# A hybrid decoder layer on one core: the chunked recurrence run as two chains without fill matmuls between its products

## The chip, the cores and the metric

The kernel runs on one core of a Trainium2 chip. The metric is the device time of one execution in microseconds (us), less is better. TensorE is shown as PE (matmuls) and PEld (weight loads), VectorE as DVE, ScalarE as ACT, GpSimd as POOL, SyncE as SP.

## What is computed

One layer of a decoder trunk for 512 prompt tokens and 32 sample tokens (8 requests of 4 tokens), model width 1024, all in fp32. Cut to what matters:

```python
x = layer_norm(ALPHA * x + 0.5 * swiglu(x, ffn1...), ln1)
proj = x @ w_in                      # r, k, v, gates for 8 heads of 64; b, c, h of the convolution
# RWKV-7, per head, token by token:
sa = einsum("bhij,bhj->bhi", s, -kk_t)
s  = s * w_t[:, :, None, :] + sa[..., None] * (kk_t * a_t)[:, :, None, :] + v_t[..., None] * k_t[:, :, None, :]
o_t = einsum("bhij,bhj->bhi", s, r_t)
# group norm of o per head, plus a bonus term, times a gate; next to it a gated convolution of width 3
mix = concat([y_rwkv, y_conv]) @ w_out
x = layer_norm(ALPHA * x + mix, ln2)
x = layer_norm(ALPHA * x + 0.5 * swiglu(x, ffn2...), ln3)
```

The sample tokens start from a given state `s` per request; the prompt starts from zero. The final states of both are outputs, next to y.

## The kernel before

**Fill work.** The large products (`mm3`, L145 to L153) split both operands into a high and a low fp32r part and issue three matmuls for each 128x128 block of weights, L149 to L151, over 256 or 288 token columns (the halves of the 544 tokens). A 128x1024 weight tile is split by ACT (L133) and DVE (L134). These products are written as generators that yield after every two blocks. A deque `bg` holds the generators that are waiting, and `take(need)` (L157) draws from its front until the yielded costs add up to `need`. `weave(key, crit)` runs a critical generator and, each time that it yields a cost, takes `FILL[key]` times that cost from `bg`. So the fill's products stand on TensorE's queue between those of the critical generator; `until`, `need` and `drain` take fill until a condition is met or the deque is empty. The engines run their instructions in the order in which a scheduler has put them from this program order.

**The recurrence.** It is written in chunks of 64 tokens. Eight heads form four pairs, and two pairs a group `g`; in a pair, the heads `par` = 0 and 1 lie on partitions 0 to 63 and 64 to 127 (`R(par)`), and `pl` is the pair's place in the group. For each group:

- `Pair.scores` (L888) forms the products of each chunk's keys with themselves and with the queries (into `SC`), transposes keys and values (into `BK` and `UV`), and writes the 64x64 blocks to memory (`Ad`).
- `elim(g)` (L933) inverts the triangular 64x64 blocks. The 16x16 diagonal blocks of all chunks are inverted by 15 short steps on DVE (L951, L953), after a round trip through memory that regroups them, and sent back through memory (L956 to L960). Then four rounds of small products (L987) build the whole inverse `XT`; each round has three pieces (chunks 0 to 3, 4 to 7, and the sample), and after each piece the generator yields 300, so that fill is woven in. After round 0, POOL copies `AR` into `SC` (L1013).
- `chain(g)` (L1018) goes through the eight chunks in order. Both pairs share a PSUM tile at each step: products of `SC` with the state S (L1033, L1035), a copy W by ACT (L1037), products with `XT` (L1048), copies into `UV` by DVE (L1049) and ACT (L1050), products with `BK` (L1055). Then DVE adds the old state (L1064) and multiplies by the chunk's decay `Pe` (L1066), for each of the two partition halves. The outputs come from L1043 and L1071 and are copied to `O` by ACT (L1073). Three times a chunk the generator yields 1000.
- `sample(g)` (L1077) does the same for the 32 sample tokens: 32 products of eight columns for S0 times `AR` (L1089), three small groups (L1103, L1110, L1117), and the update of the eight states by four products of 128x512 (L1127), each behind a masked copy `ux` by DVE (L1124), followed by two DVE operations of 128x512 per pair (L1129, L1130).
- `gnorm(g, h)` (L1134) normalizes half h of the output, with fp32 products at L1143, L1148 and L1160.

**The order of the stages** (L1254 to L1396). With fill woven in throughout: the scores of pairs 0 and 1, `elim(0)` (key e0; pair 3's projections are put into the deque behind the DVE steps), chain 0 (c0) with `sample(0)` alternating with the fill, the two halves of `gnorm(0)`, the scores of pairs 2 and 3, `elim(1)` (e1), chain 1 in parts (c1, c2, c3) with `sample(1)`, with the output projection's products (`wout(0)`, `last(0)`), with the second half of the convolution (`conv_last`) as fill, and with the first half of the second layer norm beside its last steps. The second feed-forward part follows.

Of the kernel before, what the change touches and what calls it, by code (L numbers as in the profile page):

```python
# [19 lines left out]
P = 128  # L20
# [26 lines left out]
FILL = dict(l1a=1.754, l1b=0.752, p0=9022, s0=0.93, p1=5506, s1=1.832, e0=0.658, c0=0.233, g0=0.399, s2=0.531, p3=425, s3=0.85, e1=0.392, c1=0.963, c2=0.734, c3=0.8, l2a=1.0, l2b=1.4, l3a=1.35)  # L47
# [14 lines left out]
def body(ctx: ExitStack, tc: tile.TileContext, xT, gu1, wd1, win, wo_c, wo_0, wo_1, gu2, wd2, lora, w0, vec, cst,  # L62
# [92 lines left out]
    bg = deque()  # L155

    def take(need):  # L157
        while need > 0 and bg:
            g = bg[0]
            try:  # L160
                need -= next(g)
            except StopIteration:
                bg.popleft()
# [630 lines left out]
    BK = tl([P, 2, 2, NC_, 64], F32, name="BK")  # L794
# [10 lines left out]
    POOL.memset(XT, 0.0)  # L805
    Ad = dr.tile([2, 16, 65, 64], F32, name="Ad")
# [6 lines left out]
    class Pair:  # L813
# [74 lines left out]
        def scores(self):  # L888
            p, pl, bkb, nk, vf = self.p, self.pl, self.bkb, self.nk, self.v
            AR, bv = ARs[p // 2], bvs[p // 2]  # L890
# [13 lines left out]
            for a0c, n in ((0, 5), (5, 4)):  # L904
                qs = (sm(), sm())
                for c in range(n):
                    for par, q in enumerate(qs):
                        PE.transpose(q[:, c * 64:(c + 1) * 64],
                                     bkb[R(par), a0c + c, par:par + 2, :].rearrange("p s t -> p (s t)"), ident[R(par), :])
                for par, q in enumerate(qs):  # L910
                    ACT.activation(BK[:, pl, par, a0c:a0c + n, :], s64(q[:, :64 * n]), AF.Copy)
                qs = (sm(), sm())
                for c in range(n):
# [6 lines left out]
                    PE.transpose(qs[1][R(0), d], vf[R(1), t:t + 64], ident[R(1), :])  # L920
                for par, q in enumerate(qs):
                    o = R(1 - par)
                    ACT.activation(UV[o, pl, par, a0c:a0c + n, :], s64(q[o, :64 * n]), AF.Copy)
                yield 500
# [8 lines left out]
    def elim(g, mid=None):  # L933
# [6 lines left out]
        dma(AT, diag(Ad))  # L940
        POOL.memset(De, 0.0)
# [22 lines left out]
        yield 15000 if g else 6000  # L964
        pieces = (range(0, 4), range(4, 8), range(8, 9))
        for rnd in range(4):
            for x in pieces:
# [22 lines left out]
                if rnd == 0:  # L990
                    for pr in (slice(0, 32), slice(64, 96)) if sam else (slice(0, P),):
                        ACT.activation(DM[pr, cc, :, 0:nn], qv[pr], AF.Copy)
                    yield 300
                    continue
                if rnd == 1 and not sam:
                    DVE.tensor_copy(XT[:, cc, :, 0:16], DT[:, cc, :, 0:16])
                    DVE.tensor_tensor(XT[:, cc, :, 16:64], qv, DT[:, cc, :, 16:64], op=OP.add)
                    yield 300
# [10 lines left out]
                yield 300  # L1009
# [8 lines left out]
    def chain(g, cp):  # L1018
        S = Sn = None
        tl = cp.tile  # L1020
        AR = ARs[g]
        for c in range(8):
            if c < 7:
                Sn = tl([P, 2, 2, 64], F32, name="S", bufs=2)
                for par in range(2):
                    POOL.tensor_copy(Sn[R(1 - par), :, par, :], UV[R(1 - par), :, par, c + 1, :])
            q = sm()
            for pl in range(2):
                for par in range(2):
                    dst = q[R(par), pl * 64:pl * 64 + 64]  # L1030
                    if c == 0:
                        o = R(1 - par)
                        PE.matmul(dst, SC[o, pl, par, c, 0:64], UV[o, pl, par, c, :], start=True, stop=True)  # L1033
                    else:
                        PE.matmul(dst, SC[:, pl, par, c, 0:64], S[:, pl, par, :], start=True, stop=True)  # L1035
            W = tl([P, 2, 64], F32, name="W", bufs=2)
            ACT.activation(W, v2(q), AF.Copy)  # L1037
            yield 1000
            q2 = sm()
            if c:  # L1040
                for pl in range(2):
                    for par in range(2):
                        PE.matmul(q2[R(par), pl * 64:pl * 64 + 64], S[R(par), pl, par, :], AR[R(par), pl, c, 1, :],  # L1043
                                  start=(pl == 0), stop=False, skip_group_check=True)
            q = sm()
            for pl in range(2):
                for par in range(2):
                    PE.matmul(q[R(par), pl * 64:pl * 64 + 64], XT[R(par), c, pl, :], W[R(par), pl, :], start=True, stop=True)  # L1048
            DVE.tensor_copy(UV[R(0), :, 0, c, :], v2(q, R(0)))  # L1049
# [430 lines left out]
```

## Time and profile before

| | us |
|---|---|
| median of 3 runs | 1111.46 (1110.05 to 1112.29) |
| profiled execution, whole | 1113.33 |
| its span, first to last instruction | 1111.6 |
| TensorE (PE) occupied | 1096.3 |
| DVE / ACT / POOL busy | 835.6 / 590.4 / 172.9 |
| mean granted TensorE clock | 0.994 of full |
| inverse of group 0 (L987) | 489.4 to 511.4 |
| chain 0 with its sample part | 511.4 to 556.9 |
| inverse of group 1 | 614.9 to 635.0 |
| chain 1 with its sample part | 635.0 to 692.0 |

The page gives the busy time of each engine, the slices of the span, and the chain of work that ended last. A window of the trace lists busy time and number of instructions of each engine in a stretch, the clock that TensorE was granted (1.00 is full speed) and what the DMA engines did. A row of the timeline is start, length, engine, line, operation, output and inputs, shapes and count; in brackets the idle time of the engine before it and what ended it. The records of TensorE overlap: a matmul's record begins before its predecessor's has ended, so the distance of two starts is what one costs when they are dense.

### The profile page before, as it was taken

Reading aid. Unit: us, or ns where it says so; the run is one execution under the profiler, and the core shown is the slowest. Engines: PE = TensorE matmul, PEld = TensorE weight load, DVE = VectorE, ACT = ScalarE, POOL = GpSimd, SP = SyncE. Lnnn points to the kernel's source line nnn. Section 1 sums busy time; section 2 is a strip of 40 time slices with the busy share of each in tenths; the row PEclk is TensorE's granted clock in tenths of the full one; section 3 lists DMA queues with packets and bytes.
Section 4 is the critical chain, followed back from the end, with each engine's and each line's share of the span. In section 5 each row is a group of like instructions: output and inputs, shape, how many; then the busy total and the mean of one; then the engine's idle time right before and its main releaser. Section 6 shows DMA issues by size and latency. Waiting matters only on the chain.

```text
span 1111.6 us, 22987 instructions
## 1 busy us (share of the span) xinstructions
PE 1096.3 (99%) x9330; PEld 1044.8 (94%) x9330; DVE 835.6 (75%) x1555; ACT 590.4 (53%) x1084; POOL 172.9 (16%) x283
## 2 busy tenths in 40 slices
PE   8999999999999999999999999999999999999997
PEld 8999999999999999898789878999999999999996
DVE  7797888889766757754578467887988888897665
ACT  6646555564543585652345334767555555645524
POOL 0131221312100022230000200001212213121000
PEclk9999999999999999998999999999999999999999
DMA  8567594967752342251137522553675949677402
GB/s 284 127 137 188 121 222 100 212 148 162 179 136 88 95 135 68 53 124 58 42 97 199 151 75 82 171 171 77 131 191 125 223 98 211 152 155 183 119 1 81
DMA packets 99370, 149.32 MB, mean 134 GB/s; under 512 B 35264, under 2 KB 60736, under 8 KB 99264
## 3 DMA queue, kind: packets, MB, share of 16 engines
q1 hardware_dynamic: 72064, 111.67, 32.5%
q0 software_dynamic: 27200, 36.18, 21.1%
q8 instruction: 73, 1.20, 0.4%
q14 instruction: 33, 0.27, 0.1%
HBM read 129.17 MB, written 9.75 MB: 125 GB/s over the span
## 4 chain that ended last, share of the span: by engine, by line
PE 83%; issue 6%; DVE 3%; DMA 3%; ACT 3%; POOL 1%; SPq 0%; POOLq 0%; DVEq 0%; ACTq 0%
PE mm L149 10%; PE mm L151 9%; PE mm L150 9%; PE mm L508 8%; PE mm L509 8%; PE mm L510 7%; PE sm L510 6%; PE sm L509 5%; PE sm L508 5%; PE sm L987 1%; DMA z<-sv 1%; PE sm L149 1%; PE sm L150 1%; PE sm L151 1%; DMA z<-cpb 1%
## 5 line engine op out<-in xcount | busy, mean ns | idle before, releaser
L134 DVE TENSOR_TENSOR hl<-raw,hl 128x1024 fp32r<-128x1024 f32 (+3 forms) x232 | 270.6, 1172 | 72.6 <-ACT hl L133 71.8
L133 ACT ACTIVATE hl<-raw 128x1024 fp32r<-128x1024 f32 (+3 forms) x232 | 232.0, 1013 | 78.6 <-DVE raw L475 38.0
L149 PE MATMUL mm<-xhl,hl 128*128 128x288 f32 (+1 forms) x736 | 225.2, 306 | 0.3 <-DVE z L1354 0.3
L150 PE MATMUL mm<-xhl,hl 128*128 128x288 f32 (+1 forms) x736 | 214.8, 292 | 0.0
L151 PE MATMUL mm<-xhl,hl 128*128 128x288 f32 (+1 forms) x736 | 214.6, 292 | 0.2 <-DVE hl L134 0.2
L149 PEld LDWEIGHTS mm<-xhl,hl 128*128 128x128 f32 x736 | 138.8, 189 | 8.5 <-issue 2.6
L151 PEld LDWEIGHTS mm<-xhl,hl 128*128 128x128 f32 x736 | 138.6, 189 | 4.0 <-issue 1.6
L150 PEld LDWEIGHTS mm<-xhl,hl 128*128 128x128 f32 x736 | 139.1, 189 | 2.9 <-DVE xhl L138 0.4
L510 PE MATMUL sm<-xhl,hl 128*128 128x272 f32 x432 | 125.3, 290 | 0.0
L509 PE MATMUL sm<-xhl,hl 128*128 128x272 f32 x432 | 124.5, 288 | 0.0
L508 PE MATMUL sm<-xhl,hl 128*128 128x272 f32 x432 | 124.0, 287 | 0.0
L508 PE MATMUL mm<-tv,hl 128*128 128x272 f32 x288 | 83.0, 288 | 2.4 <-ACT cpb L575 1.6
L510 PE MATMUL mm<-tv,hl 128*128 128x272 f32 x288 | 83.4, 290 | 0.0
L509 PE MATMUL mm<-tv,hl 128*128 128x272 f32 x288 | 83.2, 289 | 0.0
L481 POOL DMA_DIRECT2D raw<-in_gu x36 | 43.4, 1206 | 255.2 <-DVE hlb L138 162.1
L508 PEld LDWEIGHTS sm<-xhl,hl 128*128 128x128 f32 x432 | 81.4, 188 | 0.0
L510 PEld LDWEIGHTS sm<-xhl,hl 128*128 128x128 f32 x432 | 81.3, 188 | 0.0
L509 PEld LDWEIGHTS sm<-xhl,hl 128*128 128x128 f32 x432 | 81.2, 188 | 0.0
L487 POOL DMA_DIRECT2D raw<-in_wd x32 | 39.2, 1465 | 253.0 <-DVE hlb L138 221.4
L508 PEld LDWEIGHTS mm<-tv,hl 128*128 128x128 f32 x288 | 54.3, 189 | 3.2 <-ACT cpb L575 2.0
L508 PE MATMUL mm<-hhl,hl 128*128 128x272 f32 x192 | 56.9, 302 | 0.0
L508 PE MATMUL sm<-hhl,hl 128*128 128x272 f32 x192 | 55.8, 291 | 0.0
(381 smaller groups left out, 2835.1 us busy)
## 6 DMA issues: line engine op xcount, KB each, us to landing
raw<-in_gu SPq DMA_DIRECT2D x84, 512.0 KB, 4.6
raw<-in_gu POOLq DMA_DIRECT2D x36, 512.0 KB, 6.5
raw<-in_wd SPq DMA_DIRECT2D x32, 512.0 KB, 4.9
raw<-in_win SPq DMA_DIRECT2D x26, 512.0 KB, 3.7
raw<-in_wd POOLq DMA_DIRECT2D x32, 256.0 KB, 6.4
raw<-in_wd SPq DMA_DIRECT2D x16, 384.0 KB, 3.3
z<-cpb POOLq DMA_DIRECT2D x16, 272.0 KB, 8.8
z<-sv POOLq DMA_DIRECT2D x16, 272.0 KB, 7.0
```

Of the source, the lines that this page charges most:

```text
L133: ACT.activation(hl[:, 0, a:b], raw[:, a:b], AF.Copy)
L134: DVE.tensor_tensor(hl[:, 1, a:b], raw[:, a:b], hl[:, 0, a:b].bitcast(F32), op=OP.subtract)
L149: PE.matmul(out, wh, src[:, 0, k, c0:c1], start=(start and i == 0), stop=False)
L150: PE.matmul(out, wh, src[:, 1, k, c0:c1], start=False, stop=False)
L151: PE.matmul(out, wl, src[:, 0, k, c0:c1], start=False, stop=(stop and i == n - 1))
L481: POOL.dma_start(x.rearrange("p (s c) -> p s c", s=2), bass.AP(tensor=a11.tensor, offset=a11.offset, ap=[[2 * D, P], [P * 2 * D, 2], [1, 5 ...
L487: POOL.dma_start(four(x)[:, i], bass.AP(tensor=a11.tensor, offset=a11.offset, ap=[[DFF, P], [P * DFF, 2], [1, 256]]), accum_op=OP.add)
L508: PE.matmul(out, wh, src(0, i), start=(first and i == 0), stop=False, skip_group_check=True)
L509: PE.matmul(out, wh, src(1, i), start=False, stop=False, skip_group_check=True)
L510: PE.matmul(out, wl, src(0, i), start=False, stop=(i == n - 1), skip_group_check=True)
L987: PE.matmul(q[r0:r0 + m, o:o + nn], lhs, rhs, start=True, stop=True)
```

## The change

- **Chain.** Each pair of a group has its own PSUM tile and its own W in each chunk, and the three products of a chunk are followed by copies of 64 columns for that pair alone. Both pairs are written one behind the other, chunk by chunk. The states have three buffers instead of two, the outputs go through `big()` tiles.
- **Decay.** Instead of multiplying the state by `Pe` after each chunk, `elim` multiplies chunks 1 to 7 of `AR` by the decay of the chunk before, on POOL, one 128x896 multiplication per pair, before `AR` is copied into `SC`. In the chain the new state is one `scalar_tensor_tensor` per head: S times the decay of the chunk before, plus the product. The state of the last chunk is scaled on ACT.
- **No fill.** `recur(g)` replaces the woven chain: it draws one piece of `sample(g)` for each chunk, and from chunk 5 on one piece of `gnorm(g, 0)`, and nothing from `bg`. `bar` makes the next 24 pieces of fill be issued after the last product of the chain.
- **Inverse.** `elim` yields 0 instead of 300 between the pieces of its rounds (and 0 instead of 6000 ahead of them for group 0). `pair3` takes all of `own_a(3)` before the rounds start.
- **Packed sample.** The keys and values of the sample are also transposed into `BS` and `UP`, two heads on top of each other, by six more small products and four more ACT copies per pair in `scores`. The update of the eight states is one 128x512 product per pair instead of two.
- **Order.** The convolution is ended before chain 1; `wout(0)` goes on as fill, `last(0)` and `gnorm(1, 1)` follow chain 1, then `wout(1)` with the second layer norm. The table load written out in `gnorm` is gone.

The diff, cut to its core:

```diff
+    bar = dict(e=None, n=0)
...
     def take(need):
...
             try:
-                need -= next(g)
+                with ExitStack() as st:
+                    if bar["n"]:
+                        bar["n"] -= 1
+                        st.enter_context(tc.issue_after(bar["e"].ins))
+                    need -= next(g)
...
     def elim(g, mid=None):
...
         dma(AT, diag(Ad))
+        for pl in range(2):
+            x = AR[:, pl, 1:8].rearrange("p c x t -> p c (x t)")
+            POOL.tensor_tensor(x, x, Pe[:, 2 * g + pl, 0:7, None].to_broadcast([P, 7, P]), op=OP.mult)
...
-        yield 15000 if g else 6000
+        yield 15000 if g else 0
...
-                yield 300
+                yield 0
...
     def chain(g, cp):
...
+                Sn = tl([P, 2, 2, 64], F32, name="S", bufs=3)
...
             for pl in range(2):
+                q = sm()
                 for par in range(2):
+                    k = slice(0, P) if c else R(1 - par)
+                    PE.matmul(q[R(par), 0:64], SC[k, pl, par, c, 0:64], S[:, pl, par, :] if c else UV[k, pl, par, c, :],
+                              start=True, stop=True)
+                W = tl([P, 64], F32, name=f"W{pl}")
+                ACT.activation(W, q[:, 0:64], AF.Copy)
+                for par in range(2):
+                    PE.matmul(q[R(par), 64:128], XT[R(par), c, pl, :], W[R(par), :], start=True, stop=True)
+                DVE.tensor_copy(UV[R(0), pl, 0, c, :], q[R(0), 64:128])
+                ACT.copy(UV[R(1), pl, 1, c, :], q[R(1), 64:128])
+                for par in range(2):
+                    PE.matmul(q[R(par), 128:192], BK[:, pl, par, c, :], UV[:, pl, par, c, :], start=True, stop=True)
+                for par in range(2):
+                    dst = Sn[R(par), pl, par, :] if c < 7 else SF[R(par), pl, :]
+                    if c:
+                        DVE.scalar_tensor_tensor(dst, S[R(par), pl, par, :], Pe[R(par), 2 * g + pl, c - 1:c],
+                                                 q[R(par), 128:192], op0=OP.mult, op1=OP.add)
...
+            yield e
+        dma(wkvp_o[:, 2 * g:2 * g + 2, :], SF)
+
+    def recur(g, cp):
+        sam, gn = sample(g, cp), gnorm(g, 0, cp)
+        for c, e in enumerate(chain(g, cp)):
+            next(sam, None)
+            if c > 4:
+                next(gn, None)
+        bar.update(e=e, n=24)
+        for x in (sam, gn):
+            for _ in x:
+                pass
...
-            for par in range(2):
-                ux = tl([P, NSEQ, 64], F32, name="ux")
...
-                PE.matmul(q[R(par), :], BK[:, pl, par, 8, :], ux.rearrange("p b i -> p (b i)"), start=True, stop=True)
+            ux = tl([P, NSEQ, 64], F32, name="ux")
+            DVE.tensor_tensor(ux, UP[:, pl, None, :].to_broadcast([P, NSEQ, 64]),
+                              bmask[:, :, None].to_broadcast([P, NSEQ, 64]), op=OP.mult)
+            yield 900
+            PE.matmul(q, BS[:, pl, :], ux.rearrange("p b i -> p (b i)"), start=True, stop=True)
...
     def pair3():
         need(2, 2)
         bg.appendleft(own_a(3))
+        need(3, 1)
...
-    bg.appendleft(alt(sample(0, cp), bg.popleft()))
-    weave("c0", chain(0, cp))
-    weave("g0", seq(gnorm(0, 0, cp), gnorm(0, 1, cp)))
+    recur(0, cp)
+    weave("g0", gnorm(0, 1, cp))
...
     weave("e1", elim(1))
+    until(lambda: fin)
...
-    weave("c1", islice(ch, 12))
...
+    recur(1, cp)
+    bg.append(last(0))
+    weave("g1", gnorm(1, 1, cp))
     drain()
     bg.append(wout(1))
-    weave("c3", alt(seq(ch, gnorm(1, 1, cp)),
-                    (n * FILL["l2a"] for n in layer_norm(z, *HALF[0], V_LN2G, V_LN2B, epsl, lnq, lnr, f2.s1[0], to_x(False)))))
+    weave("l2a", layer_norm(z, *HALF[0], V_LN2G, V_LN2B, epsl, lnq, lnr, f2.s1[0], to_x(False)))
```

125 lines of the change are left out of this document (50 added, 75 removed).

## Prediction

> **What bounds the kernel now.** I read the page first (busy time, the slices, the chain of work that ended last), then the windows of the stages that the change touches, then the timeline inside them.
>
> ```profile
> span 1111.6 us, 22987 instructions
> PE 1096.3 (99%) x9330; PEld 1044.8 (94%) x9330; DVE 835.6 (75%) x1555; ACT 590.4 (53%) x1084; POOL 172.9 (16%) x283
> PE 83%; issue 6%; DVE 3%; DMA 3%; ACT 3%; POOL 1%; SPq 0%; POOLq 0%; DVEq 0%; ACTq 0%
> ```
>
> TensorE is occupied 99% of the span and is 83% of the chain that ends last. So the kernel ends when TensorE has got through its list, and the question is how many microseconds of TensorE's time the recurrence takes. Windows of four stages (inverse and chain of group 0, then of group 1) and of the stretch behind them, first for all work, then for the fill matmuls into the mm tiles alone; columns are window, length, busy time and count of PE, PEld, DVE, ACT (POOL), then granted clock, DMA share and GB/s:
>
> ```profile
> 489.40:511.40 22.00, 22.00 (x375) 18.97 (x374) 9.62 (x25) 11.38 (x26) 5.57 (x15) 1.00 0.24 56
> 511.40:560.20 48.80, 48.62 (x534) 38.41 (x533) 24.76 (x63) 14.37 (x40) 3.63 (x14) 0.90 0.23 74
> 614.90:635.00 20.10, 20.10 (x361) 17.34 (x360) 8.15 (x20) 6.15 (x13) 3.17 (x8) 1.00 0.46 118
> 635.00:692.00 57.00, 56.93 (x629) 46.34 (x628) 37.77 (x95) 23.26 (x55) 3.00 (x10) 1.00 0.29 93
> 692.00:740.00 48.00, 47.57 (x331) 44.71 (x331) 43.46 (x74) 30.75 (x49) 0.00 (x0) 1.00 0.51 171
> ...
> 489.40:511.40 22.00, 11.97 (x73) 9.58 (x72) 0.46 (x2) 2.48 (x8) 1.00 0.24 56
> 511.40:560.20 48.80, 23.16 (x116) 16.99 (x115) 0.92 (x3) 0.80 (x2) 0.90 0.23 74
> 614.90:635.00 20.10, 12.87 (x73) 9.81 (x72) 0.94 (x3) 0.41 (x1) 1.00 0.46 118
> 635.00:692.00 57.00, 34.01 (x209) 26.98 (x208) 5.79 (x15) 0.00 (x0) 1.00 0.29 93
> ```
>
> Busy time is occupancy: records overlap. What a fill matmul costs when packed densely is the distance of two starts:
>
> ```profile
> 493.08 0.28 PE L149 MATMUL mm<-xhl,hl 128*128 128x256 f32 x1
> 493.21 0.28 PE L150 MATMUL mm<-xhl,hl 128*128 128x256 f32 x1
> 493.32 0.28 PE L151 MATMUL mm<-xhl,hl 128*128 128x256 f32 x1
> ...
> 494.28 1.24 PE L842 MATMUL sm<-kq,cs 128*128 128x256 f32 x4
> ...
> 500.39 1.16 PE L851 MATMUL sm<-cs,sw 128*128 128x128 f32 x8
> ```
>
> The first three starts lie 0.24 us apart, 0.12 us each with 256 columns; with 288 it is 288/256 of that, 0.13 us. So dense fill would have taken 72 x 0.126 = 9.1 us of the first window, 115 x 0.124 = 14.3 of the second, 72 x 0.128 = 9.2 of the third and 207 x 0.12 = 24.8 of the fourth (the means follow the mix of the two widths). The rest is what the recurrence costs TensorE today: 22.0 - 9.1 = 12.9, 48.8 - 14.3 = 34.5, 20.1 - 9.2 = 10.9, 57.0 - 24.8 = 32.2 us. In the first, about 2.0 us are pair 3's own fp32 products (the last two rows, 1.24 and 1.16 us, their overlapping tails off), which only move to another place; 10.9 stays. **Together 88.5 us.** The fill itself is not changed (as many matmuls after as before), so the new time is the old one minus 88.5 plus what inverse and chain take alone, plus what the displaced fill loses.
>
> **The change part by part.**
>
> *Chain.* The instruction order of the changed kernel has no fill matmul between the first and the last product of either chain, and the products of pair 0 and pair 1 alternate. A step therefore lasts as long as one pair's path from state to state. Its pieces stand in these rows (timeline; start, length, engine, line):
>
> ```profile
> 516.03 0.22 DVE L1095 COPY SC<-sm 64x64 f32<-64x64 f32 x1 [0.60 <-PE sm L1089]
> 516.28 0.21 ACT L1095 COPY SC<-sm 64x64 f32<-64x64 f32 x1 [0.56 <-DVE SC L1095]
> 516.50 0.23 ACT L1098 ACTIVATE WT<-sm 128x64 f32<-128x64 f32 x1
> ...
> 533.52 0.45 PE L1048 MATMUL sm<-W,XT 64*64 64x64 f32 x8
> 534.02 0.28 DVE L1049 COPY UV<-sm 64x128 f32<-64x128 f32 x1 [0.58 <-PE sm L1048]
> 534.34 0.26 ACT L1050 COPY UV<-sm 64x128 f32<-64x128 f32 x1 [1.29 <-DVE UV L1049]
> 534.95 0.34 PE L1055 MATMUL sm<-UV,BK 128*64 128x64 f32 x4
> ```
> ```profile
> L1179 DVE SCALAR_TENSOR_TENSOR zc<-cu,vc,zc 128x32 f32<-128x32 f32 x4 | 1.0, 248 | 0.0
> ```
>
> A pair's product group (two products, 4 records, as each fp32 product leaves two) lasts 0.34 us; its three copies 0.23 (128x64 on ACT), 0.22 (64x64 on DVE) and 0.21 (64x64 on ACT, behind DVE's, as in before); the new state needs two scalar_tensor_tensor of 0.25 us behind each other (nearest row: 128x32). Hand-overs: 0.05 from PE to DVE (533.52 + 0.45 to 534.02) and 0.04 between DVE and ACT; I take 0.1 from PE to ACT. Sum: 3 x 0.34 + 0.23 + 0.22 + 0.21 + 2 x 0.25 + some 0.4 of hand-overs = **2.58 us a step** at full clock. The other pair fits into its gaps: DVE has 4 x 0.25 + 2 x 0.22 = 1.4 us a step, ACT about 1.5 with the copies of W, UV and the outputs. Today's decay pass (one DVE multiplication of 0.29 us per head) is off the path.
>
> Half clock is the open size. The clock was halved once inside the trace, in chain 0:
>
> ```profile
> 513.55:516.97 3.42, 3.29 (x81) 3.25 (x81) 1.82 (x7) 0.70 (x3) 0.24 (x2) 1.00 0.75 232
> 516.97:520.40 3.43, 3.43 (x23) 2.67 (x22) 0.98 (x4) 0.28 (x1) 0.00 (x0) 0.50 0.01 5
> ...
> 527.20:530.60 3.40, 3.40 (x58) 2.91 (x56) 1.28 (x4) 1.29 (x4) 0.61 (x2) 1.00 0.00 0
> 636.40:639.80 3.40, 3.40 (x82) 3.20 (x81) 2.22 (x7) 1.05 (x4) 0.00 (x0) 1.00 0.38 151
> ```
> ```profile
> 523.70 0.69 PE L1048 MATMUL sm<-W,XT 64*64 64x64 f32 x8
> 525.58 0.49 PE L1055 MATMUL sm<-UV,BK 128*64 128x64 f32 x4
> ...
> 513.73 1.10 PE L1089 MATMUL sm<-AR,DM 64*64 64x8 f32 x32
> ```
>
> The halving from 516.97 to 527.2 follows a window in which TensorE was occupied 3.29 of 3.42 us, but by 8 fill matmuls and 72 small ones, most of them 8 columns wide. So in this trace it is little streaming, not long gaps, that goes before the halving (a like window at 636.4 had no such sequel, so it stands near the edge). A chain without fill streams less still: 40 records of 64 columns in a step of 2.6 us, no wide one among them. I take half clock for three windows in four; then a group of 4 takes 0.49 for 0.34 us, the step 3.03, the mean step 2.92.
>
> The Trainium skill, page "TensorE: Matmul & The Clock Gate", section "HAM oscillation — how this bites in real kernels", speaks of avoiding idle gaps of TensorE over about 3.4 us. By that rule no gap of a chain (each under 1 us here) would halve the clock and the sum would be that of the first rival below; the row at 513.55 speaks against reading it so.
>
> *What else stands in a chain.* The sample's 8-column products (32 records in 1.10 us) wait for the state's load, the first row below (4.1 us from issue to landing), and stand ahead of chunk 1's products in TensorE's queue (chain 0) or inside chunk 0 (chain 1): about 1.7 us. Beside them stand the packed products, gnorm's, and DVE operations of 128x512 between those of the state:
>
> ```profile
> DM<-in_s SPq DMA_DIRECT2D x1, 512.0 KB, 4.1
> ```
> ```profile
> L1124 DVE TENSOR_TENSOR ux<-UV,cs 128x512 f32<-128x512 f32 x4 | 2.7, 687 | 0.0
> 538.95 1.07 PE L1127 MATMUL sm<-ux,BK 128*64 128x512 f32 x2
> ```
>
> The two remaining 128x512 products are two records of 0.43 us each (1.07 for two, the tail off): 1.7, half of it in gaps of the chain: 0.9; six DVE operations of 0.69, each in the way of a state by 0 to 0.69: 1.3; four products of gnorm, half as wide, so again 1.7 and 0.9. Together 4.8 at full clock; 5.6 as the clock mixes. Chunk 7 has no successor (-0.6); behind the last product TensorE still waits for a DVE and an ACT result before the fill (+1.7). **A chain: 8 x 2.92 + 5.6 - 0.6 + 1.7 = 30 us** (26.4 at full clock). Halving the packed products saves two of 0.86 us per group, which lie in the 34.5 and 32.2 already; six more small products and four ACT copies per pair in the scores cost some 0.3 us of TensorE a pair by the 0.34 us group, which I leave out (0 to 2 us in all).
>
> *Inverse.*
>
> ```profile
> 490.62 2.08 PE L987 MATMUL sm<-DM,SC 64*64 64x64 f32 x62
> 498.17 2.06 PE L987 MATMUL sm<-O,DM 64*64 64x48 f32 x60
> 502.84 0.70 PE L987 MATMUL sm<-XT,DM 64*32 64x32 f32 x32
> 507.30 0.57 PE L987 MATMUL sm<-XT,DM 64*16 64x16 f32 x32
> ```
>
> Inverse 0 in one piece: 2.08 + 2.06 + 2 x 0.70 + 2 x 0.57 and four sample groups of about 0.2 are 7.5; half a microsecond for copies that nothing covers: **8** (7.3 to 9). Inverse 1 keeps fill between its products in the instruction order: **10.5** (10 to 11).
>
> *Decay into AR.* Two POOL multiplications of 128x896 per group. No row has one; the nearest is
>
> ```profile
> L1013 POOL COPY SC<-AR 64x512 f32<-64x512 f32 x8 | 5.9, 742 | 3.6 <-PE sm L987 3.3
> ```
>
> 1.45 ns an element, so 1.3 us each from below and, read twice, 2.6 from above. They stand at the start of the inverse, ahead of POOL's small copies for pair 3's projections and of the SC copies behind round 0; the 15 DVE steps and the round trip through memory behind them cover them. I take 0, between 0 and 3 us a group if POOL's library reload in front of the first is long.
> The Trainium skill, page "GPSIMD Engine Reference", section 3.1, gives 4497 ns for 2048 elements, an estimate of 2.0 us for one of these; the sum would not change.
>
> *Side losses.* Fill that ran in chain 1 now follows it, in a stretch where DVE is busy 43.46 of 48 us already: a late weight tile or two there, 3 us (0 to 6). The first fill behind each chain may still run at half clock, up to 1.7 us each (half a window): 1.5 for both. **4.5.**
>
> **Sum:** 8 + 30 + 10.5 + 30 + 4.5 = 83.0 us instead of 88.5: -5.5. The profiled execution took 1113.33 us (span 1111.6 and 1.7 around it): 1107.8. It lay 1.9 us above the median of the runs shown, 1111.46, so against that median **1106.0**.
>
> **The rivals.**
>
> *Full clock in the chains.* For it: the window at 636.4, and the 40 records a step are wider than those at 513.7. Then 7.3 + 26.4 + 10 + 26.4 + 3 = 73.1, or -15.4: 1096.
>
> *Slower: half clock from the inverse into the fill.* One mechanism: too little streaming keeps the clock halved in every window, at the 3.03 us step plus the hand-overs that grow with it, so 3.3, and with extras of 7: chains 8 x 3.3 + 7 - 0.6 + 1.7 = 34.5 at worst, 33.5 taken; inverses 9 + 11; 7 behind them: 94, or +5.5: 1117. It decides from a chain of (88.5 - 8 - 10.5 - 4.5) / 2 = 32.75 us, a step of about 3.25. For it: the clock went low in before with fill still in the chain. Against it: a halving lasted 10.2 us and ended by itself although the fill between was thin.
>
> *The pairs don't overlap.* If one pair's copy stands behind the other's waiting operation in ACT's or DVE's queue, a step nears twice its length; half way there it is 4.4 us, a chain 8 x 4.4 + 6.7 = 41.9, and the sum 106.8: +18, 1130. The alternating order speaks against it.
>
> *The gain is given back.* POOL's multiplications or DVE behind chain 1 hold fill up by another 3 us each: between -1 and +2, near 1112. For it: DVE at 91% there.
>
> *It does not do what it says* would be fill left in the chains; the instruction order excludes that, except in inverse 1, where I count none of it.
>
> **How the numbers follow.** Forecast -5.5 (1101 to 1110): 0.38. Full clock: 0.22. Half clock throughout: 0.22. No overlap: 0.04. Given back: 0.14. A measurement tells about 0.2%, 2 us, from no change. Faster: 0.36 + 0.22 = 0.58; within 0.2%: 0.10; slower: 0.22 + 0.04 + 0.06 = 0.32. The range takes in both clock cases, 1093 to 1118.
>
> **What would show it.** In the changed profile: windows over the two chains of 26 to 34 us with no mm matmul in them; starts of one pair's products of successive chunks 2.6 (full clock) or 3.0 us (half) apart; granted clock 0.5 in most of those windows; 128x64 groups of 0.34 or 0.49 us; inverse 0 in 8 us; DVE as releaser of TensorE's idle time behind chain 1. The forecast is wrong if the step is over 3.25 us, if the clock stays at 1.00 in the chains, or if TensorE's idle time outside the four windows grows by more than 5 us.

## The result, and the profile after

The changed kernel takes **1152.01 us** (median of 4 runs, 1146.59 to 1155.54) where the kernel before takes 1111.88 (1110.05 to 1120.87): a ratio of 1.0345, 95% interval 1.0302 to 1.0388. It is slower by 40 us; 1106 were predicted. The profiled execution took 1152.78. For the experiments below, the kernel before was run again beside them, with medians of 1114.30 to 1115.71 us. Medians are over all runs; the ratios leave out two long ones, one of ten of `b_both` (2641.82 us) and one of four of `a_fill1` (1162.72 us).

The page of the changed kernel: span, busy time by engine, granted clock in 40 slices, and the chain that ended last by engine.

```profile
span 1151.0 us, 23188 instructions
...
PE 1130.4 (98%) x9362; PEld 1072.8 (93%) x9362; DVE 834.4 (72%) x1569; ACT 599.7 (52%) x1156; POOL 179.3 (16%) x288
...
PEclk9999999999999999985789958999999999999999
...
PE 82%; issue 6%; DVE 4%; DMA 4%; ACT 3%; SPq 1%; POOL 1%; DVEq 0%; POOLq 0%; ACTq 0%
```

TensorE is still occupied 98% of the span and still carries the chain. New are two dips of the clock, at the places of the two chains. The windows of inverse 0, chain 0, inverse 1 and chain 1, columns as in the prediction; the last line is chain 0 again with the matmuls of L149 alone (a third of the fill):

```profile
501.00:509.93 8.93, 7.75 (x289) 7.06 (x288) 5.79 (x15) 3.69 (x9) 3.80 (x7) 0.96 0.26 68
509.93:560.56 50.63, 49.99 (x413) 35.99 (x411) 16.29 (x57) 13.76 (x60) 2.29 (x8) 0.50 0.03 11
...
623.21:662.48 39.27, 39.26 (x522) 37.34 (x522) 17.65 (x43) 12.62 (x26) 5.21 (x16) 1.00 0.44 131
662.48:707.46 44.98, 43.76 (x412) 31.52 (x412) 19.08 (x60) 15.20 (x64) 2.29 (x8) 0.62 0.09 25
...
509.93:560.56 50.63, 0.00 (x0) 0.00 (x0) 0.50 0.03 11
```

The chains hold no fill, as planned, and last 50.6 and 45.0 us instead of the 30 forecast, at a clock of 0.50 and 0.62. To see where all of the 39.4 us went, I cut both traces at the first and last product of each stage and took off each stage's length its fill matmuls (0.118 us each with 256 columns, 0.132 with 288, the distances of dense starts). What is left is what the stage costs TensorE beside its fill:

| stage | before | after | difference |
|---|---|---|---|
| end of the first feed-forward part to inverse 0 | 35.5 | 39.3 | +3.8 (2.0 moved here from inverse 0) |
| inverse 0 | 13.0 | 8.9 | -4.0 |
| chain 0 | 32.4 | 50.6 | +18.2 |
| between chain 0 and inverse 1 | 18.9 | 24.4 | +5.6 |
| inverse 1 | 11.0 | 10.0 | -1.0 |
| chain 1 | 32.3 | 45.0 | +12.7 |
| behind chain 1, to the second feed-forward part | 11.9 | 15.5 | +3.6 |
| the rest | | | +0.6 |

Three quarters of the loss lie in the two chains. Two things hide in their rows: before's 32.4 us hold some 5.1 us lost to its own halving (half of the 10.2 us that it lasted, an estimate), and each chain of the changed kernel holds seven records of the group norm's products (1 in before's chain 0, 12 in its chain 1), some 4 us at half clock. For the chains, the rows of before, cut in the same way, and the clock of the changed kernel in the windows in which it changes:

```profile
511.41:557.22 45.81, 45.63 (x518) 35.98 (x518) 23.85 (x60) 11.81 (x36) 3.62 (x14) 0.89 0.20 62
635.05:688.99 53.94, 53.87 (x602) 43.33 (x602) 34.84 (x86) 23.01 (x55) 3.00 (x10) 1.00 0.27 87
```
```profile
509.18:563.79 54.61, 53.45 (x422) 38.71 (x421) 19.03 (x63) 15.12 (x64) 2.29 (x8) 0.50 0.04 11
594.51:601.34 6.83, 6.83 (x44) 5.41 (x43) 1.80 (x3) 2.49 (x10) 0.00 (x0) 0.50 0.32 45
```
```profile
560.37:563.79 3.42, 3.42 (x13) 2.66 (x9) 2.93 (x8) 1.35 (x4) 0.00 (x0) 0.50 0.01 2
563.79:567.20 3.41, 3.39 (x23) 2.92 (x22) 2.08 (x6) 2.24 (x5) 0.38 (x2) 1.00 0.67 248
...
666.19:700.32 34.13, 33.36 (x259) 24.13 (x258) 11.46 (x41) 9.70 (x44) 2.29 (x8) 0.50 0.04 13
```

The clock is halved from 509.18 to 563.79 without a break, although TensorE is occupied 53.45 of these 54.61 us; and it stays so for a window behind the chain, in which fill already runs (13 records, then 23 in the next window at full clock). Another halving, 594.51 to 601.34, lies in the scores of pairs 2 and 3. Half of these two stretches, 1.7 and 3.4 us, would be most of the +5.6 between chain 0 and inverse 1 (an estimate).

One step of chain 0 (chunk 2): DVE's timeline from one state update to the next, and the first part of TensorE's timeline between them.

```profile
519.52 1.22 DVE L1077 SCALAR_TENSOR_TENSOR S<-S,Pe,sm 64x64 f32<-64x64 f32 x4 [0.69 <-PE sm L1073]
...
524.33 1.22 DVE L1077 SCALAR_TENSOR_TENSOR S<-S,Pe,sm 64x64 f32<-64x64 f32 x4 [0.40 <-PE mm L1087]
```
```profile
519.85 0.47 PE L1064 MATMUL sm<-S,SC 128*64 128x64 f32 x2
520.25 0.47 PE L1084 MATMUL mm<-AR,S 64*64 64x64 f32 x2
520.65 0.47 PE L1064 MATMUL sm<-S,SC 128*64 128x64 f32 x2
521.06 0.47 PE L1084 MATMUL mm<-AR,S 64*64 64x64 f32 x2
521.46 0.47 PE L1064 MATMUL sm<-S,SC 128*64 128x64 f32 x2
521.87 0.48 PE L1069 MATMUL sm<-W,XT 64*64 64x64 f32 x4
522.27 0.47 PE L1064 MATMUL sm<-S,SC 128*64 128x64 f32 x2
522.68 0.48 PE L1084 MATMUL mm<-AR,S 64*64 64x64 f32 x4
523.12 0.48 PE L1069 MATMUL sm<-W,XT 64*64 64x64 f32 x4
```

The step takes 524.33 - 519.52 = 4.81 us, and TensorE waits for nothing in this list: each start follows the one before by 0.40 to 0.44 us. The reader should see two things. The output products (L1084) stand between the products of the path (L1064). And one head's product (2 records) takes 0.40 us by itself, as long as two heads' products (4 records) that run side by side on the two halves of the array.

ACT's list has a wait of the same kind. DVE's half of the first pair's copy into UV ended at 522.68, but ACT's half began at 523.09, behind the other pair's W, which had to wait for TensorE:

```profile
522.85 0.22 ACT L1067 ACTIVATE W<-sm 128x64 f32<-128x64 f32 x1 [1.40 <-PE sm L1064]
523.09 0.21 ACT L1071 COPY UV<-sm 64x64 f32<-64x64 f32 x1
```

The steps of chunks 2 to 4 take 4.8 to 5.4 us (one pair's state updates at 519.52, 524.33, 529.73 and 534.53). The last three take 6.2 to 8.9 (the updates that follow come at 540.69, 548.28 and 557.19). Two of them:

```profile
540.69 0.59 DVE L1077 SCALAR_TENSOR_TENSOR S<-S,Pe,sm 64x64 f32<-64x64 f32 x2 [0.82 <-PE sm L1073]
...
548.28 0.61 DVE L1077 SCALAR_TENSOR_TENSOR S<-S,Pe,sm 64x64 f32<-64x64 f32 x2
```

They lie 7.59 us apart, and the other pair's update stands alone between them, at 544.33. Besides the chain's products TensorE's list holds here two records of the sample's product of 128x512 (2.0 us, 545.57 to 547.57), and in the steps before and behind it two and four records of the group norm (1.15 us for two). So of chain 0's 50.6 us, 9.6 lie ahead of the update at 519.52, 15.0 are the next three steps, and 26.0 are the last three and what follows them.

### The profile page after: what moved, and what is told of

Its sections match the earlier page's. It is cut to its first block, busy times and chain, and to the rows that moved or that the text cites. A ratio compares the mean times of both kernels' runs of the same rounds, so it can differ in the third digit from the quotient of the medians.

```text
span 1151.0 us, 23188 instructions
## 1 busy us (share of the span) xinstructions
PE 1130.4 (98%) x9362; PEld 1072.8 (93%) x9362; DVE 834.4 (72%) x1569; ACT 599.7 (52%) x1156; POOL 179.3 (16%) x288
## 4 chain that ended last, share of the span: by engine, by line
PE 82%; issue 6%; DVE 4%; DMA 4%; ACT 3%; SPq 1%; POOL 1%; DVEq 0%; POOLq 0%; ACTq 0%
PE mm L149 9%; PE mm L150 8%; PE mm L151 8%; PE mm L513 8%; PE mm L514 7%; PE mm L515 7%; PE sm L515 5%; PE sm L514 5%; PE sm L513 5%; PE mm L1084 1%; PE sm L1064 1%; ACT hl L133 1%; PE sm L1016 1%; PE mm L1087 1%; PE sm L150 1%
## 5 line engine op out<-in xcount | busy, mean ns | idle before, releaser
L149 PE MATMUL mm<-xhl,hl 128*128 128x288 f32 (+1 forms) x736 | 219.5, 299 | 2.5 <-ACT hl L133 2.5
L150 PE MATMUL mm<-xhl,hl 128*128 128x288 f32 (+1 forms) x736 | 213.4, 290 | 0.0
L151 PE MATMUL mm<-xhl,hl 128*128 128x288 f32 (+1 forms) x736 | 212.2, 290 | 0.0
L149 PEld LDWEIGHTS mm<-xhl,hl 128*128 128x128 f32 x736 | 138.9, 189 | 7.5 <-ACT hl L133 3.2
L492 POOL DMA_DIRECT2D raw<-in_wd x32 | 39.3, 1465 | 280.6 <-DVE hlb L138 249.0
```

What stands on the lines that cost most here:

```text
L149: PE.matmul(out, wh, src[:, 0, k, c0:c1], start=(start and i == 0), stop=False)
L150: PE.matmul(out, wh, src[:, 1, k, c0:c1], start=False, stop=False)
L151: PE.matmul(out, wl, src[:, 0, k, c0:c1], start=False, stop=(stop and i == n - 1))
L492: POOL.dma_start(four(x)[:, i], bass.AP(tensor=a11.tensor, offset=a11.offset, ap=[[DFF, P], [P * DFF, 2], [1, 256]]), accum_op=OP.add)
```

## The experiments

**Which products make the step.** `a_noout` drops the output products, and O copies another column range:

```diff
-                for par in range(2) if c else ():
-                    PE.matmul(o[R(par), 0:64], S[R(par), pl, par, :], AR[R(par), pl, c, 1, :], ...)
-                for par in range(2):
-                    e = PE.matmul(o[R(par), 0:64], UV[:, pl, par, c, :], SC[:, pl, par, c, 64:128], ...)
-                ACT.activation(O[:, pl, c, :], o[:, 0:64], AF.Copy)
+                ACT.activation(O[:, pl, c, :], qq[pl][:, 128:192], AF.Copy)
```

> The changed kernel without the output products of the chain (both groups of 64-column products that feed O are left out, O gets a copy of another PSUM column range, so the output y is not the reference's). In the changed kernel a step takes 4.8 us at half clock, where 40 records lie 0.107 us apart. Theory RATE: at half clock TensorE's own streaming bounds the step, 40 x 0.107 = 4.3 us plus the sample's records. With 24 records it is 2.6, less than the path of 3.0, so a step falls by 1.3 to 1.8 us, 16 steps by 20 to 28 us: about 1127 us, clock still 0.5 in the chains. Rival PATH (copies, hand-overs and the order of the two pairs' products set the step, the outputs are beside it): 0 to 6 us less, 1146 to 1152 us.

One run: 1131.56 us, 20 less than the changed kernel. The state updates of chain 0, at clock 0.50:

```profile
518.10 1.22 DVE L1079 SCALAR_TENSOR_TENSOR S<-S,Pe,sm 64x64 f32<-64x64 f32 x4 [0.26 <-PE sm L1075]
...
521.84 1.31 DVE L1079 SCALAR_TENSOR_TENSOR S<-S,Pe,sm 64x64 f32<-64x64 f32 x4 [0.18 <-PE sm L1075]
```

A step is 3.74 us instead of 4.81. PATH falls: the outputs were not beside the step. RATE's time is just reached, but its step isn't: 1.07 us went where it had 1.3 to 1.8, and in this step TensorE waits three times, 0.23, 0.37 and 0.22 us, the longest for the second pair's W:

```profile
520.85 0.48 PE L1071 MATMUL sm<-W,XT 64*64 64x64 f32 x4 [0.37 <-ACT W L1069]
```

So with the outputs TensorE's list fills the step, and without them it doesn't. Some of the 20 us came from the clock, which was halved for a shorter time (to 550, and 652.6 to 676.4 and 679.9 to 686.7).

**One pair alone.** `a_one` runs the first pair's chain only (`for pl in range(1)`, its O and final state copied for the second); `a_one_d` adds wide products as below, 6 a chunk.

> The changed kernel with one pair of each group in the chain: the products, copies and states of the second pair are left out, and its part of O and of the final state is a copy of the first pair's, so the outputs that hang on it are not the reference's. It runs at half clock as far as I can tell, with 20 records a step, 2.1 us of TensorE. If the working of the prediction is right for one pair by itself, a step takes 3.0 us at half clock (between two states of the same pair), and what the second pair adds to reach 4.8 is its share of TensorE and of the copies' engines. If a single pair also takes 3.7 us or more, the path itself was costed too low. Whole time 1118 to 1130 us.

> The same single pair, with products of 128x256 that nobody reads behind each chunk, 16 behind chunks 0 and 1 and 6 behind the others, to hold the clock at 1.00. Theory LOCKSTEP (both pairs wait for the same engines at the same time, DVE's four state operations and two copies a step, ACT's six): a single pair's step at clock 1.00 is 2.5 to 2.7 us, as predicted, against 3.2 to 3.6 for two. If it is 3.0 us or more the hand-overs were costed too low. In both cases some 0.1 to 0.7 us of a step can be the 6 wide products in front of the next chunk's; the step is read where they do not stand in the path. Whole time 1112 to 1125 us.

`a_one` took 1133.09 us, `a_one_d` 1138.69 (one run each), both above what was expected. A step of `a_one` at half clock, DVE's and TensorE's timeline:

```profile
517.83 0.59 DVE L1077 SCALAR_TENSOR_TENSOR S<-S,Pe,sm 64x64 f32<-64x64 f32 x2 [0.77 <-PE sm L1073]
...
521.51 0.59 DVE L1077 SCALAR_TENSOR_TENSOR S<-S,Pe,sm 64x64 f32<-64x64 f32 x2 [0.88 <-PE sm L1073]
```
```profile
518.16 0.47 PE L1064 MATMUL sm<-S,SC 128*64 128x64 f32 x2 [0.23 <-DVE S L1077]
518.57 0.47 PE L1084 MATMUL mm<-AR,S 64*64 64x64 f32 x2
518.97 0.47 PE L1064 MATMUL sm<-S,SC 128*64 128x64 f32 x2
...
520.68 0.47 PE L1087 MATMUL mm<-SC,UV 128*64 128x64 f32 x2 [0.39 <-DVE UV L1070]
520.93 0.48 PE L1073 MATMUL sm<-UV,BK 128*64 128x64 f32 x4
```
```profile
520.66 0.21 ACT L1071 COPY UV<-sm 64x64 f32<-64x64 f32 x1 [0.90 <-DVE UV L1070]
```

3.68 us, where 3.03 were worked out. The difference is in the rows. An output product stands in the path from 518.57 to 518.97 (0.40). Another stands from 520.68 to 520.93, but it delays nothing: the product behind it needs ACT's copy, which ended at 520.87, and starts 0.06 later. That leaves 3.68 - 0.40 = 3.28, and 0.25 that the prediction costed too low: by the rows, 0.59 for the two state operations instead of 0.50, and about 0.6 for the hand-overs instead of 0.4. Put together (an estimate from three runs): 3.28 for one pair's path, 0.46 more with the second pair (`a_noout`'s 3.74), 1.07 more with the outputs. `a_one_d` settles little: at full clock its step was 3.71 us (state updates at 523.71 and 527.42), but wide products stand in the path. So at full clock LOCKSTEP isn't shown; at half clock the 0.46 us, with TensorE waiting, are a sign of it.

**Does wide work hold the clock?** `a_dummy4` and `a_dummy16` add products of 128x256 that nobody reads at the end of each chunk, 4, or 16 behind chunks 0 and 1 and 4 behind the others:

```diff
+            o = big()
+            for _ in range(16 if c < 2 else 4):
+                PE.matmul(o[:, 0:256], xhl[:, 0, 4, 0:128], xhl[:, 0, 5, 0:256], start=True, stop=True)
             S = Sn
             yield e
```

> The changed kernel with four products of 128x256 (fp32r, into a PSUM tile that nobody reads) at the end of each chunk, 64 in all, 7.7 us of TensorE at full clock. Theory RATE with the clock following wide streaming: the clock stays at 1.00 in most of the two chains, a step takes 2.6 to 3.1 us instead of 4.8, the chains lose 2 x 13 to 2 x 18 us: 1116 to 1126 us. If the halving does not depend on wide streaming: clock 0.5 as before and 64 x 0.21 us more, about 1165 us. Rival PATH: the clock does not matter much; 1152 to 1160 us.

> The changed kernel with products of 128x256 that nobody reads at the end of each chunk: 16 behind chunks 0 and 1, where the sample's load is waited for, 4 behind the others, 56 per chain, 6.7 us at full clock. With 4 per chunk chain 1 kept clock 1.00 and chain 0 was halved at chunk 1. If wide streaming over the wait keeps the clock up, both chains are at 1.00, the clock is also up behind chain 0, and the time is about 1122 to 1130 us (a chain of 32 us and the dummies on top). What the changed kernel is worth at full clock is this less some 10 us for the dummies: theory LOCKSTEP (the two pairs move together, so that a step is 3.2 us and not 2.58): no gain on before, 1110 to 1116. Rival of the prediction, a step of 2.58 at full clock: 1096 plus the dummies, below 1110 as run.

`a_dummy4`: 1143.27 us (one run; 1116 to 1126 were expected). `a_dummy16`: 1132.89, ratio to before 1.0165 (1.0085 to 1.0244), a little above the expected 1130. Chain 0 and chain 1 of each:

```profile
510.04:561.39 51.35, 50.43 (x442) 36.87 (x439) 16.30 (x57) 13.76 (x60) 2.30 (x8) 0.56 0.04 12
661.20:696.87 35.67, 33.81 (x440) 25.22 (x440) 19.03 (x60) 15.04 (x64) 2.30 (x8) 1.00 0.10 32
```
```profile
509.59:551.84 42.25, 40.62 (x466) 32.16 (x464) 16.10 (x56) 13.60 (x61) 2.30 (x8) 0.88 0.04 14
648.68:689.78 41.10, 38.40 (x464) 30.01 (x464) 19.02 (x60) 14.84 (x64) 2.29 (x8) 0.92 0.09 28
```

More work on TensorE makes the kernel 9 and 19 us faster: the clock is what the chains lack. With 4 products a chunk it held in chain 1 and not in chain 0; with 16 over the wait for the sample's load it held in most of both. The second thing to see is chain 1 of `a_dummy4`, the only chain of the changed form at clock 1.00 from end to end with nothing but such products added: 35.67 less 29 x 0.12 (29 of its 32 lie inside) = **32.2 us**. Before's chain 1 costs TensorE 32.3 beside its fill. At full clock the chain without fill gains nothing; 26.4 were forecast. Take 112 x 0.12 = 13.4 us from `a_dummy16` and 1119.5 are left; half of the 17.1 us that its chains still ran at half clock would make it some 1111 (an estimate), no gain on before either.

**Real fill instead.** `a_fill1` and `a_fill2` draw one or two pieces of fill in each chunk of `recur` (`take(1)` behind `next(gn, None)`).

> The changed kernel, but each chunk of a chain draws one piece of fill (six matmuls, 0.72 us dense) behind its output products. Theory RATE: if six wide matmuls in a step of 3.3 us hold the clock at 1.00, each chain costs TensorE some 27 us beside its fill instead of 45 to 50, and the clock is also up behind it: 1098 to 1110 us. If they don't hold it in all windows, 1110 to 1135. Rival PATH: the fill is put between the products and the step stays; 1140 to 1150 us.

> As the run with one piece of fill for each chunk, with two (twelve matmuls, 1.44 us). Theory RATE: the clock is at 1.00 in nearly all of both chains; a step takes about 4.0 us, 1.44 of them fill; 1096 to 1108 us, and no slower than with one piece. Rival PATH: 1135 to 1148 us.

`a_fill1`: 1152.07 us (1142.33 to 1162.72), ratio 1.0363 (1.0295 to 1.0431); `a_fill2`: 1132.19, ratio 1.0152 (1.0107 to 1.0197). Both expectations were missed: the times are far above RATE's; `a_fill1` lies at PATH's upper end, `a_fill2` below PATH's 1135. Chain 0 and 1 of `a_fill1`, then of `a_fill2`:

```profile
510.42:574.74 64.32, 63.17 (x462) 44.99 (x457) 20.36 (x65) 16.30 (x64) 2.87 (x12) 0.55 0.07 20
664.94:701.72 36.78, 36.26 (x456) 27.78 (x456) 19.15 (x61) 15.36 (x64) 2.71 (x8) 1.00 0.15 45
```
```profile
509.93:551.41 41.48, 40.99 (x501) 31.97 (x497) 20.99 (x65) 16.77 (x66) 2.94 (x12) 1.00 0.15 47
641.57:689.17 47.60, 46.96 (x499) 36.95 (x499) 23.61 (x68) 17.65 (x66) 2.28 (x8) 0.86 0.19 57
```

Six wide matmuls a chunk were on the edge: chain 0 was halved at 517.19 and did not recover, chain 1 kept full clock. With 47 and 88 fill matmuls taken off, the two chains at clock 1.00 cost 31.2 (`a_fill1`, chain 1) and 30.5 us (`a_fill2`, chain 0): again no gain, as woven chains cost 32.3 (before's chain 1) or 27.7 and 30.2 (`b_both`, below) at that clock.

**Is it the sample's narrow products?** In both kernels 64 records of 8 columns stand where the clock falls. `a_samplate` puts the sample behind the chain, among fill:

```diff
-        sam, gn = sample(g, cp), gnorm(g, 0, cp)
+        gn = gnorm(g, 0, cp)
...
-    weave("g0", gnorm(0, 1, cp))
+    weave("g0", seq(late(sample(0, cp)), gnorm(0, 1, cp)))
```

> The changed kernel with the sample part put behind the chain, among fill, instead of into it. If the 64 records of 8 columns at the start of the chain are what starts the halving (they stand in the window ahead of it in before and in the changed kernel alike): the clock is 1.00 in both chains, a step takes 3.2 to 3.3 us, a chain 28 us instead of 45 to 50: 1112 to 1125 us. If the chain's own 40 records of 64 columns in a step are too little: 0.5 through both chains, a step 4.3 to 4.8 us, and 1140 to 1152 us.

1165.17 us, ratio 1.0446 (1.0349 to 1.0542): above both expected ranges, with the clock of the second.

```profile
511.25:556.28 45.03, 44.34 (x326) 32.36 (x323) 12.70 (x49) 13.54 (x57) 2.30 (x8) 0.51 0.04 12
662.56:708.74 46.18, 44.02 (x324) 32.01 (x323) 15.54 (x53) 14.97 (x60) 2.30 (x8) 0.54 0.08 24
```

The chain's own products are too little: 0.51 and 0.54 without any 8-column product. Chain 0 is 5.6 us shorter than with the sample in it, chain 1 is 1.2 longer at its lower clock, and the sample costs more than that outside.

**The parts alone, on the kernel before.** `b_elim`: the inverse yields 0 and pair 3 is taken first. `b_packed`: the packed sample. `b_both`: these two. `b_chain`: the new chain and the moved decay, with three yields a chunk and fill as before.

> The kernel before with one part of the change alone: the inverse yields 0 between the pieces of its rounds, and pair 3's projections are taken ahead of the rounds. If the inverse in one piece is worth what the changed kernel's trace shows (TensorE beside its fill 8.9 us for 13.0 in group 0, of which 2 only moved, and 10.0 for 11.0 in group 1): 1107 to 1110 us. Rival: inverse without fill streams little, the clock halves in chain 0 earlier and for longer than the 10 us of before, and takes it back: 1112 to 1120 us.

> The kernel before with the packed sample alone. Two products of 128x512 less per group (0.86 us each) are 3.4 us less of TensorE, the products added in the scores 0.5 to 2 us more: 1108 to 1111 us against 1111.9. Rival: the added ACT copies and the longer wait of one product for one ux cost as much as is saved: 1112 to 1115 us.

> The kernel before with the two parts that did no harm alone, the inverse in one piece and the packed sample, and its woven chain and order of stages. If their savings add up in TensorE's time (3 us of inverse less 1 to 2 given back, and up to 3 us of packed products less 1 in the scores): 1106 to 1111 us against 1112 to 1114. If the halving in chain 0 comes earlier with an inverse without fill: 1111 to 1117, no difference.

> The kernel before with the changed chain alone (each pair its own PSUM tile and copies of 64 columns, decay moved into AR on POOL, scalar_tensor_tensor for the new state), with the fill woven in at three yields a chunk as before. Theory CLOCK AND RATE (the loss comes from the fill that is missing: the clock halves, and at half clock 40 records a step are TensorE's bound): this kernel stays near before, 1108 to 1118 us, clock 1.00 in most of both chains. Rival FORM (the loss is in the chain's own form: twice as many copies, four scalar_tensor_tensor a step, outputs in big tiles that the fill needs): 1125 us or more.

| kernel | median us | ratio to before (95%) |
|---|---|---|
| `b_elim` | 1112.45 | 0.9982 (0.9954 to 1.0010) |
| `b_packed` | 1116.73 | 1.0006 (0.9971 to 1.0042) |
| `b_both` | 1112.50 | 0.9961 (0.9934 to 0.9988) |
| `b_chain` | 1128.22 | 1.0118 (1.0053 to 1.0183) |

Inverse and packing alone make no difference that can be told, so the savings expected of each weren't seen; together they are the one version whose interval lies below 1, by 0.1 to 0.7%. The chain does harm even when woven. Its rows, chain 0 and 1 of `b_chain`, then of `b_both`:

```profile
512.99:568.90 55.91, 55.91 (x491) 40.16 (x491) 23.47 (x68) 14.57 (x61) 4.23 (x12) 0.76 0.15 49
650.00:707.73 57.73, 57.53 (x602) 45.17 (x602) 35.32 (x94) 26.17 (x81) 3.95 (x8) 0.97 0.25 82
```
```profile
511.49:555.31 43.82, 43.77 (x542) 35.49 (x538) 23.19 (x61) 13.67 (x38) 3.63 (x14) 1.00 0.19 68
631.51:682.26 50.75, 50.73 (x590) 41.66 (x587) 34.63 (x86) 23.10 (x57) 3.61 (x12) 1.00 0.28 86
```

In chain 1, with as many fill matmuls as before (181) and the clock at 0.97, `b_chain` costs 36.0 us beside its fill for 32.3; in chain 0 (80 fill matmuls for 108, clock 0.76) 45.9 for 32.4. Half of the halved time, taken as the clock's share, is 1.7 us in `b_chain`'s chain 1 (3.4 us halved), 13.7 in its chain 0 (27.3) and 5.1 in before's chain 0 (10.2). What is left, 34.3 for 32.3 and 32.2 for 27.3, puts the form at some 2 to 5 us a chain (an estimate). So neither expectation held alone. In `b_both`, which has the packed sample too and clock 1.00 in both chains, the old chain costs 27.7 and 30.2 us beside its 130 and 170 fill matmuls: in chain 0 that is nearly the 26.4 that were forecast for the new chain without fill. With more fill (`b_chain_c0`, next) the new chain costs 7 us more than `b_c0`, which keeps the old one. What of the form, the larger number of copies or the order of the heads' products, wasn't tried.

**More fill in chain 0.** `b_c0`, `b_packed_c0` and `b_chain_c0` set the fill factor of chain 0 to 0.7 (`c0=0.7` for `c0=0.233`).

> The kernel before with one number changed: the fill factor of chain 0 is 0.7 instead of 0.233, so that 169 fill matmuls stand in chain 0 instead of 108. Theory: wide streaming holds the clock; the halving of 10 us in chain 0 goes, which costs TensorE 4 to 5 us there: 1106 to 1109 us against 1112 to 1114. Rival: the halving is started by the 64 records of 8 columns whatever stands beside them, or more fill in the chain only lengthens it: no difference, 1111 to 1116.

> The kernel before with the packed sample and the fill factor 0.7 in chain 0 (168 fill matmuls). If both parts hold: clock 1.00 in chain 0, two products of 0.86 us less per group: 1104 to 1109 us. If the packing is worth nothing outside a lucky window: as the run with the factor alone.

> The changed chain alone in the kernel before, woven, with the fill factor 0.7 in chain 0 (156 fill matmuls instead of 79). With the factor 0.233 it had clock 0.5 for 27 us of chain 0. Theory CLOCK: with the clock up, chain 0 costs 32 to 34 us beside its fill instead of 46, and the time is 1110 to 1117 us; what stays above the run with the factor alone is the form's own cost. Rival FORM: 1122 us or more with the clock at 1.00.

1124.65 us (ratio 1.0097, 1.0066 to 1.0128), 1118.97 (1.0034, 1.0005 to 1.0062) and 1131.62 (1.0143, 1.0084 to 1.0202): all missed; `b_chain_c0` came out at FORM's time, but not at its clock, which was halved for 13.7 us in each chain. The halved windows of `b_c0`:

```profile
518.21:521.62 3.41, 3.41 (x22) 2.99 (x18) 0.78 (x3) 0.43 (x2) 0.00 (x0) 0.50 0.00 0
675.22:682.05 6.83, 6.45 (x42) 4.35 (x40) 1.88 (x6) 4.03 (x9) 0.00 (x0) 0.50 0.32 97
726.42:733.25 6.83, 5.93 (x23) 5.71 (x24) 6.20 (x8) 3.68 (x4) 0.00 (x0) 0.50 0.58 178
```

The halving in chain 0 shrank from 10.2 to 3.4 us and the chain from 32.4 to 29.3 us beside its fill, a little less than the 4 to 5 expected. But two new ones came, in chain 1 and behind it: chain 1 cost 39.1 us for 32.3, the stretch behind it 17.8 for 11.9. The one in chain 1 lies in a stretch of 12 us without a single fill matmul (670.64 to 682.87), which before's chain 1 doesn't have. That the fill taken early was missing there, since one deque serves all stages, is likely but not shown: the whole chain had more of it, 205 matmuls for 181.

## Why the prediction was wrong

- *What bounds the kernel, and 88.5 us as the recurrence's price:* right; the account above, by the same method, gives the whole difference. Of the 88.5, about 5 us (an estimate) were lost to before's own halving in chain 0.
- ***"A step therefore lasts as long as one pair's path from state to state"*: this step failed.** I counted three product groups of one pair, 12 of its 20 records, and took the other pair and the output products to lie in gaps. The outputs stand on TensorE's list between the products of the path (0.40 us for one pair at half clock). With two pairs and outputs there are no gaps: the list of 40 records fills a step, 4.81 us at half clock, and 6.2 to 8.9 in the last three chunks, where the group norm's and the sample's products stand on it too. The 3.03 us are nearly right for one pair without outputs (3.68 - 0.40 = 3.28), which is not what runs.
- *"The other pair fits into its gaps":* I gave DVE's and ACT's share of a step, not TensorE's, the engine that bounds the kernel. The row of 4 records in 0.34 us misled me besides: it holds when two heads run side by side. In the changed order many products of one head stand alone and cost 0.40 us at half clock.
- *The pairs don't overlap*, given 0.04: part of its mechanism was there. ACT's copy for one pair stood behind the other's waiting W, and began 0.41 us after DVE's half had ended. Its price, 41.9 us a chain and 1130, is the nearest of all, but by luck: it left the outputs off TensorE's list too.
- *Half clock "for three windows in four":* it was all of chain 0 and 34 of 45 us of chain 1. The direction held, and the reason, little wide streaming, is borne out by `a_dummy16` and `a_samplate`. The slower rival had the mechanism, half clock into the fill, but with the step of 3.3 us its price was 33.5 us a chain, where 50.6 and 45.0 came. The prediction gave the slower cases 0.32 together, and its whole range ended at 1118.
- *The full-clock rival, 1096:* refuted as a price. Chains at clock 1.00 cost 30.5 to 32.2 us, not 26.4 (its terms add up to 26.5), so that even a kept clock would have left the change near before.
- The Trainium skill's rule against idle gaps of TensorE over about 3.4 us ("TensorE: Matmul & The Clock Gate", "HAM oscillation — how this bites in real kernels") does not reach this case: the clock was halved for 54.6 us while TensorE was occupied 53.45 of them. The trace doesn't agree with reading it as enough to avoid gaps.
- *Extras of 5.6 us a chain:* too low. `a_samplate`'s chain 0 is 5.6 us shorter, but without the sample alone; the group norm's seven records cost some 4 us more at half clock (1.15 for two). That the two numbers are the same is chance.
- *Inverse:* 8.9 and 10.0 us for 8 and 10.5; right.
- *Decay on POOL, hidden:* right. Three of the four took 1.68 us, one 2.38, all between the bounds of 1.3 and 2.6, and nobody waited for one. The view by line, of the two in group 1:

```profile
L969 POOL TENSOR_TENSOR AR<-AR,Pe 128x896 f32<-128x896 f32 x2 | 3.4, 1684 | 5.9 <-PE sm L911 5.9
```

- *Side losses of 4.5:* 5.6 between the chains (the clock's tail and the halving in the scores) + 3.6 behind chain 1 + 1.8 ahead of inverse 0 (3.8 less the 2.0 moved) = 11. The late weight tile behind chain 1 was there; TensorE waited 2.5 us for ACT's half of such tiles, not DVE's.

What stays open: how much wide work a window needs for the clock to stay (six wide matmuls a chunk held it in one chain and not in the other); what of it counts, since the unread products are wider, use more of the array and fill short waits all at once; and which part of the new chain's form costs its 2 to 5 us when it is woven.

## What to carry to other kernels

Here fill between the products of a latency chain did two things: it used the waits, and it kept the clock up. When you cost its removal, list everything that the busiest engine issues in a step, in its order, not one chain's path, and cost that list at the clock that such work had in a trace. This chain cost TensorE 28 to 32 us beside fill at full clock, and 30 to 32 with little or no fill: there was nothing left to win even with the clock kept.

## What the runs showed of the hardware

- A halving lasted 54.6 us in the changed kernel, while narrow products ran, and 10.2 in before: 16 and 3 times 3.41 us.
- TensorE's occupancy didn't tell of the halving: it was 98% of the halved stretch. Extra products of 128x256 that nobody reads made the kernel faster (1132.89 for 1152.01).
- A 64-column fp32 product of one head took 0.40 us at half clock alone, and four records of two heads side by side 0.40 to 0.44. At full clock the one alone took 0.26 (`a_one_d`, 524.03 to 524.29).
